# Stores on GpSimd's queue, and a re-ordered passage from up to down, in a hybrid mLSTM/attention block

## The chip, the cores and the metric

The kernel runs on one core of a Trainium2 chip. The metric is the device time of one execution in microseconds (us), smaller is better. The core has five engines, each with its own instruction queue that runs in order: TensorE (PE, matrix products), VectorE (DVE), ScalarE (ACT), GpSimd (POOL) and SyncE (SP). PE writes to PSUM; the others move data between PSUM and the on-chip memory, SBUF. Transfers between SBUF and device memory are done by 16 DMA engines; an engine's queue only issues them. Engines wait for each other by semaphores.

## The reference

One layer of a bidirectional encoder for 2048 tokens of width 1024, in float32:

```
xn   = rms_norm(h, ln_mix_g);  proj = xn @ w_in            # 1024 x 2512
y_a  = mlstm_group(proj[q, k, v, o, gates])                # 4 heads x 128, chunks of 128, both directions
y_b  = mla_group(proj[c_q, c_kv, k_rope])                  # attention, 4 heads, 2048 x 2048 scores each
h    = h + concat(y_a, y_b) @ w_out                        # 1024 x 1024
u    = dwconv3(rms_norm(h, ln_ffn_g) @ w_up)               # 1024 x 5632, then a 3-tap convolution along the tokens
h    = h + (silu(u[gate]) * u[val]) @ w_down               # 2816 x 1024
h    = h + sigmoid(rms_norm(h) @ w_ple_gate) * rms_norm(p @ w_ple_proj)
out  = rms_norm(h, final_g)
```

## The kernel before, in words

**Products.** Every float32 operand is split into a high part and a low part (helper `split`, L112 to L120: ACT casts, DVE subtracts), and each product is three PE passes (`mm3`, L127 to L132). PE is the busiest engine, so all else is arranged around its order.

**Stages.** `run` (L147) calls them in turn.

1. *Input projection* (`in_proj`, L180). x comes turned, in 16 tiles of 128 tokens. `load_w` loads and splits a weight strip; `load_x` (L219) loads an x tile, `split_x` splits it. For the first strip `load_w` loads three weight tiles and then has the first x tile split (`before`). Queries and keys of the mLSTM are made last, feature by feature (`block`, L374); a second stream of work, `side` (weights absorbed for attention, `q_up`), is advanced between products by `pump` (L368) at 0.96 steps a call, and what is left of it runs at the end.
2. *Attention with the mLSTM beside it* (`attend`, L943; `mlstm`, L728). Attention goes over 64 tiles (4 heads, 16 query tiles) in an order written out by hand (`order`, L982). At each dot in it a generator may be advanced by one step; the number of steps is spread evenly with `SIDE` = 613. The generator is the rest of the projection and then the mLSTM: a backward pass over chunks 15 to 1, which stores the turned keys and the state of every chunk (`kn_d`, `cb_d`), and a forward pass over chunks 0 to 15 that reads them back, masks (`affine_select` on POOL, L813), multiplies, normalises (`rsq` on POOL, L135 to L141, then DVE at L860) and stores its part of `y_d` (L867). A `yield` or `pause(n)` marks places where attention's products may go in between. Attention stores its part of `y_d` at L977, two stores for each pair of query tiles.
3. *Output projection* (`out_proj`, L1100): 16 chunks of 128 tokens: 48 products, addition to x, a store of h (`h1_d`, L1135), the norm (root on POOL), and, one chunk later, PE turns the normed tile and `transpose_out` stores it into `x2_d` (L1068; 1024 rows of 512 bytes).
4. *Up and down* (`up_down`, L1359). Both are products of 2 by 2 blocks with seven block products in place of eight (the Winograd form of Strassen's method). The operands are sums and differences: the resident ones are called B11, B21, B22 and T1 to T4 (`load_op`, L1241, loads and splits four 128x512 tiles of each; for later blocks from `t_d` and `tw_d`, where `sum4`, L1205, has stored the sums), the others A11, A12, A22 and S1 to S4 (`up_prep`, L1324). There are 44 up pairs in two blocks of NC2 = 22 (NUP = 44), then 24 down pairs in three blocks of 8. A pair's seven products go A11 by B11, S1 by T1, (rest of the pair before: A22 by T4, S4 by B22), S2 by T2, A12 by B21, S3 by T3; `rest` (L1378) is thus one pair late. `conv` (L1393) is the 3-tap convolution and gate of an up pair: ACT and DVE over two 128x1024 tiles in places w7 and w11, whose result is stored into `hid_d` (L1413, L1415). In the first down pair it comes directly behind `rest` of the last up pair (L1490), and only then are that pair's output tiles loaded (`down_out`). The sums of down's weights (`wsums`, 11 steps) are made at up pairs 28, 31, 34 and 37 and in down's first two blocks (`steps`, L1445).
5. *The per-layer gate and the final norm* (`ple`, L1547), whose preparation runs beside the last down block.

**Queues.** Every DMA, load or store, is issued by SP, so a store waits for its data in the same in-order queue as all loads. A framework decides each engine's order from the program order and its own estimates, allots SBUF by place names (`self.at("w7", ...)`), and puts in the waits for reuse of a place.

Of the kernel before, what the change touches and what calls it, by code (L numbers as in the profile page):

```python
# [19 lines left out]
P = 128  # L20
# [17 lines left out]
SIDE = 613  # L38
# [22 lines left out]
class Block:  # L61
# [118 lines left out]
    def in_proj(self):  # L180
# [6 lines left out]
        def load_w(c0, n, before=None):  # L187

            out, raws = [], []

            def load(k2):
                raw = self.at(next(rrot), [P, 2, 512], name="wraw")
                nc.sync.dma_start(raw[:, :, :n], w_in[k2, :, :, c0:c0 + n])
                raws.append(raw)

            if before:
# [22 lines left out]
        def load_x(st):  # L219

            t = self.at(next(rrot), [P, KT, P], name="x_t")
            for f in range(1 if st else 2):
                fs = slice(0, KT) if st else slice(4 * f, 4 * f + 4)
                nc.sync.dma_start(t[:, fs], d["x_turned"][:, fs, st * P:(st + 1) * P])
            return t
# [72 lines left out]
        ws = load_w(OFF_R, NREST, lambda: split_x(0, xq[0]))  # L298
# [69 lines left out]
        def pump():  # L368
            due[0] += 0.96
# [358 lines left out]
    def mlstm(self):  # L728
# [17 lines left out]
        def state(r, j, kk, v1, old, new):  # L746
# [3 lines left out]
            yield from pause(3)  # L750
# [23 lines left out]
        for c in range(NT - 1, 0, -1):  # L774
# [3 lines left out]
            nc.sync.dma_start(self.kn_d[c], kk[:, 0])  # L778
# [3 lines left out]
            nc.sync.dma_start(self.cb_d[c - 1], new)  # L782
# [3 lines left out]
        for c in range(NT):  # L786
# [3 lines left out]
            cb = self.at(f"t{4 + c % 2}", [P, NH, 129], name="cb")  # L790
            nc.sync.dma_start(cb, self.cb_d[c])
# [9 lines left out]
            if c < NT - 1:  # L801
# [65 lines left out]
            nc.sync.dma_start(self.y_d[c, :, 0:4, :], hy[:, 1])  # L867
# [75 lines left out]
    def attend(self, side):  # L943
# [18 lines left out]
        def pv(w, half):  # L962
# [10 lines left out]
            if half == 1:  # L973
                rb = self.at(f"s{pr % 3}", [P, 2, P], name="ya")
                nc.scalar.copy(rb, w.ps.rearrange("p (a t) -> p a t", a=2))
                for i in range(2):
                    nc.sync.dma_start(self.y_d[2 * pr + i, :, 4 + h, :], rb[:, i])  # L977
# [77 lines left out]
    def transpose_out(self, xn, otag, dst, two=True):  # L1055
# [12 lines left out]
        nc.sync.dma_start(dst, xo)  # L1068
# [31 lines left out]
    def out_proj(self):  # L1100
# [14 lines left out]
        for c in range(NT):  # L1115
# [19 lines left out]
            nc.sync.dma_start(self.h1_d[c], xt)  # L1135
# [69 lines left out]
    def sum4(self, src, dst, ops):  # L1205
# [16 lines left out]
        for i, t in enumerate((b12, b22, b11, b21)):  # L1222
            if not ops or i > 1:
                nc.sync.dma_start(dst(i), t)
# [77 lines left out]
    def down_out(self, i):  # L1302
# [3 lines left out]
        for e in range(2):  # L1306
# [17 lines left out]
    def up_prep(self, i):  # L1324
# [23 lines left out]
        if keep:  # L1348
            nc.sync.dma_start(self.s_d[c, 0], sv)
# [4 lines left out]
        if keep:  # L1354
            nc.sync.dma_start(self.s_d[c, 1], sg)
# [3 lines left out]
    def up_down(self, out):  # L1359
# [4 lines left out]
        L, H = slice(0, SB), slice(SB, 2 * SB)  # L1364
        NUP, blocks = self.NUP, self.BLOCKS
        self.hrot = _rot("", ("u0", "w7", "w11", "u1", "u2"))
# [11 lines left out]
        def rest(s):  # L1378

            prod(s.y, s.ops["A22"], "T4", True)  # L1380
            if s.down:
                add(s.o[1][:, L], s.o[1][:, L], s.y)
                nc.sync.dma_start(self.h2_d[2 * s.pr + 1], s.o[1])
# [3 lines left out]
            if s.down:  # L1387
                add(s.o[0][:, H], s.o[0][:, H], s.z)
                nc.sync.dma_start(self.h2_d[2 * s.pr], s.o[0])
# [3 lines left out]
        def conv(s):  # L1393
            b, c = divmod(s.i, NC2)
            ts = []
            for half, u in enumerate((s.ug, s.uv)):
# [5 lines left out]
                t = self.at(("w7", "w11")[half ^ s.i % 2], [P, 2 * SB], name="fgv")  # L1402
# [9 lines left out]
            if b:  # L1412
                nc.sync.dma_start(self.hid_d[c, :, 2 * SB - 1:4 * SB - 1], ts[0])  # L1413
            else:
                nc.sync.dma_start(self.hid_d[c, :, 0:2 * SB - 1], ts[0][:, 1:])  # L1415
# [27 lines left out]
        sums = [self.sums(1)] + [self.wsums(g) for g in range(3)]  # L1443
        steps = {}
        for q, (i0, at) in enumerate(((0, (6, 9, 12, 15)), (NC2, (6, 9, 12, 15)), (NUP, (2, 3, 4, 5)), (NUP + 8, (2, 3, 4)))):  # L1445
            for a in at:
                steps[i0 + a] = sums[q]
        ple, outs = self.ple(out), {}
        for i in range(n):
# [17 lines left out]
            prod(x, s.ops["A11"], "B11")  # L1467
            if s.down:
                s.o = outs.pop(i) if i in outs else None
            else:  # L1470
                s.p1 = self.at(f"t{6 + i % 2}", [P, SB], name="p1")
                nc.scalar.copy(s.p1, x)
            if s.down and s.o:
                add(s.o[0][:, H], s.o[0][:, H], x)
                o2 = s.o[1].rearrange("p (a t) -> p a t", a=2)
                add(o2, o2, x.unsqueeze(1).broadcast_to([P, 2, SB]))
# [9 lines left out]
            if prev:  # L1486
                rest(prev)
                if prev.i == NUP - 1:
                    conv(prev)
                    s.o = self.down_out(i)  # L1490
                    add(s.o[0][:, H], s.o[0][:, H], x)
                    o2 = s.o[1].rearrange("p (a t) -> p a t", a=2)
                    add(o2, o2, x.unsqueeze(1).broadcast_to([P, 2, SB]))
# [24 lines left out]
            load(then, "B21")  # L1518
# [3 lines left out]
            if s.down and i + 1 < n:  # L1522
                outs[i + 1] = self.down_out(i + 1)
            if prev and not s.down:
                conv(prev)
            prod(s.y, s.ops["S3"], "T3", True)
            if s.down:
# [19 lines left out]
    def ple(self, out):  # L1547
# [99 lines left out]
        for st in range(NT):  # L1647
# [15 lines left out]
            for i in range(len(cuts) - 1):  # L1663
# [9 lines left out]
                nc.vector.tensor_tensor(h2[:, fs], h2[:, fs], gfin[:, fs], op=ALU.mult)  # L1673
            st2 = self.stat(1, "ps3")
            nc.vector.tensor_reduce(st2, s2, axis=AX.X, op=ALU.add)  # L1675
            r2 = self.rsq(st2, 1, 1.0 / D)
# [51 lines left out]
```

## Time and profile before

| | |
|---|---|
| median of 3 runs | 2990.7 us (2990.33 to 2992.8) |
| the profiled execution | 2990.93 us, of which the traced span is 2989.1 us |
| granted TensorE clock, mean | 0.996 |
| DMA issued on SP's queue | 458.12 MB, 47.6% of the 16 engines' time |
| attention with the mLSTM | about 505 to 1250 us of the span |
| output projection, up, down | about 1250 to 1455, 1455 to 2296, 2296 to 2750 us |

How to read the lines that follow: a group row gives line, engine, operation, out<-in; in a timeline row the first two numbers are start and duration in us, xN is how many equal instructions were merged, and the bracket is how long the engine stood idle before, and which instruction or transfer ended the wait. A wait row reads: who <- for whom: us in total, times, longest. "fxy" and "fzs" are PSUM tiles of up and down, "op" a resident operand, "fw" a split operand of a pair, "fgv" a tile of the convolution, "hid_d" the hidden tensor in device memory. SPq is SP's issue queue; its time is that of issuing, not of moving. PEld is the loading of weights into PE, which overlaps PE.

### The profile page before, as it was taken

The numbers are of one execution on the slowest core, as the hardware profiler recorded it, in microseconds if no ns is written. First come the engines' busy times: TensorE is split into PE (matmuls) and PEld (weight loads), VectorE is DVE, ScalarE is ACT, GpSimd is POOL, SyncE is SP. The second block draws the span as 40 slices with busy tenths as digits, with TensorE's granted clock in tenths as the row PEclk, the third lists the DMA queues.
The fourth block names the chain that finished last, engine by engine and source line by source line (L and its number), as shares of the span: only waits on it lengthen the run. The fifth ranks groups of instructions, "written<-read, shape, count | busy, mean of one in ns | idle before, by whom it ended". The sixth has DMA issues, their size and how long they took to land. (4 is left out here: it accounts for less than half of the span.)

```text
span 2989.1 us, 40727 instructions
## 1 busy us (share of the span) xinstructions
PE 2917.3 (98%) x14858; PEld 2452.2 (82%) x14858; DVE 2072.1 (69%) x3798; ACT 1350.2 (45%) x2644; POOL 141.5 (5%) x262
## 2 busy tenths in 40 slices
PE   8999999999999999999999999999997999999999
PEld 7888888889889888888778887788886787877887
DVE  7431556777777777645888888877778778687665
ACT  7211544555656566523544445444445132233443
POOL 3100000000000000001000000000000000000111
PEclk9999999999999999999999999999998999999999
DMA  6522444343333333568663435744436868575221
GB/s 189 115 73 92 138 131 155 119 149 110 100 97 98 94 120 113 168 220 273 217 214 133 141 134 191 250 143 127 123 124 197 274 200 283 190 248 200 79 80 64
DMA packets 377657, 460.73 MB, mean 154 GB/s; under 512 B 30176, under 2 KB 263152, under 8 KB 377456
## 3 DMA queue, kind: packets, MB, share of 16 engines
q1 hardware_dynamic: 377456, 458.12, 47.6%
q8 instruction: 117, 1.92, 0.3%
q14 instruction: 84, 0.69, 0.1%
HBM read 294.53 MB, written 163.51 MB: 153 GB/s over the span
## 5 line engine op out<-in xcount | busy, mean ns | idle before, releaser
L130 PE MATMUL fxy<-op,fw 128*128 128x512 f32 x3168 | 751.3, 393 | 28.7 <-DVE fw L120 16.7
L130 PEld LDWEIGHTS fxy<-op,fw 128*128 128x128 f32 x3168 | 587.4, 188 | 176.2 <-DVE fh L1363 17.8
L130 PE MATMUL fzs<-op,fw 128*128 128x512 f32 x1584 | 385.9, 389 | 0.9 <-DVE xt L1134 0.9
L130 PEld LDWEIGHTS fzs<-op,fw 128*128 128x128 f32 x1584 | 297.1, 188 | 63.0 <-DVE xt L1134 1.1
L130 PE MATMUL bk<-wsp,xh 128*128 128x512 f32 (+1 forms) x768 | 234.9, 387 | 1.2 <-DVE wsp L126 1.0
L117 ACT CAST pt<-tb 128x512 fp32r<-128x512 f32 x256 | 147.1, 587 | 195.5 <-PE tb L959 195.2
L901 DVE TENSOR_REDUCE mx<-bk 128x1 f32<-128x512 f32 x256 | 174.9, 685 | 46.1 <-PE bk L900 44.9
L130 PE MATMUL ppv<-pt,kv 128*128 128x256 f32 x1536 | 203.3, 287 | 0.0
L120 DVE TENSOR_TENSOR pt<-tb,pt 128x512 fp32r<-128x512 f32 x256 | 174.1, 686 | 35.6 <-ACT pt L117 33.9
L130 PE MATMUL fxy<-op,fwd 128*128 128x512 f32 x792 | 191.8, 391 | 6.4 <-DVE fh L1363 3.4
L130 PEld LDWEIGHTS ppv<-pt,kv 128*128 128x128 f32 x1536 | 188.8, 191 | 0.0
L919 ACT ACTIVATE pe<-bk,nm 128x512 f32<-128x512 f32 x256 | 174.5, 696 | 25.5 <-DVE nm L913 24.3
L130 PEld LDWEIGHTS fxy<-op,fwd 128*128 128x128 f32 x792 | 148.0, 188 | 39.9 <-DVE fh L1363 4.9
L130 PE MATMUL pgp<-pw,x3s 128*128 128x512 f32 (+1 forms) x792 | 178.9, 385 | 0.6 <-DVE pw L120 0.6
L130 PE MATMUL bk<-wo,yhl 128*128 128x512 f32 x744 | 175.4, 392 | 0.0
L130 PEld LDWEIGHTS pgp<-pw,x3s 128*128 128x128 f32 x792 | 144.4, 188 | 29.4 <-DVE pw L120 1.1
L130 PEld LDWEIGHTS bk<-wsp,xh 128*128 128x128 f32 x768 | 144.5, 189 | 28.4 <-DVE wsp L126 3.2
L1363 DVE TENSOR_TENSOR fh<-fh,fxy 128x512 f32<-128x512 f32 (+1 forms) x144 | 109.6, 773 | 75.3 <-PE fxy L130 72.8
L130 PEld LDWEIGHTS bk<-wo,yhl 128*128 128x128 f32 x744 | 138.2, 188 | 28.1
L130 PE MATMUL bk<-wsp,xl 128*128 128x512 f32 (+1 forms) x384 | 150.8, 393 | 9.1 <-ACT wsp L125 9.0
L117 ACT CAST fw<-hraw 128x1024 fp32r<-128x1024 f32 (+1 forms) x72 | 70.5, 982 | 192.1 <-PE fxy L130 124.0
L130 PE MATMUL bk<-xh,wqk 128*128 128x512 f32 x480 | 156.8, 392 | 0.0
(325 smaller groups left out, 5019.6 us busy)
## 6 DMA issues: line engine op xcount, KB each, us to landing
fwr<-in_w_up SPq DMA_DIRECT2D x66, 512.0 KB, 4.1
fh<-h_d SPq DMA_DIRECT2D x48, 512.0 KB, 5.1
h_d<-fh SPq DMA_DIRECT2D x48, 512.0 KB, 2.8
s_d<-fwr SPq DMA_DIRECT2D x44, 512.0 KB, 3.1
fws<-s_d SPq DMA_DIRECT2D x44, 512.0 KB, 3.7
rw<-row_d SPq DMA_DIRECT2D x32, 512.0 KB, 5.1
hraw<-hid_d SPq DMA_DIRECT2D x30, 512.0 KB, 4.2
tsum<-in_w_down SPq DMA_DIRECT2D x44, 256.0 KB, 4.5
```

What stands on the lines that cost most here:

```text
L117: nc.scalar.copy(hi, src)
L120: (sub or nc.vector).tensor_tensor(lo, src, _f(hi), op=ALU.subtract)
L130: mm = lambda *a, **k: self.nc.tensor.matmul(*a, **k, skip_group_check=more)
L901: nc.vector.tensor_reduce(s.mx[:, kb:kb + 1], ps, axis=AX.X, op=ALU.max)
L919: nc.scalar.activation(s.pe[:, kb % 2], s.banks[kb], AF.Exp, bias=s.nm, scale=ASCALE, accum_out=s.rs[:, kb:kb + 1])
L1363: add = lambda o, a, b: tt(o, a, b, op=ALU.add)
```

## The change

Line numbers in the prediction are those of the kernel before. The change has these parts:

- *Stores on another queue.* The stores of the mLSTM (`kn_d`, `cb_d`, `y_d`), of attention (`y_d`), of the output projection (`h1_d`, `x2_d`), of `sum4`, of `up_prep` (`s_d`), of `conv` (`hid_d`) and of down (`h2_d`) are issued by GpSimd: 344 stores. SP keeps 970 of 1314 issues. The loads, the projection's stores and the final output stay on SP.
- *The start.* The first two weight tiles are loaded in halves, and one half of the first x tile is loaded and split behind each of them; x's first tile has a place of its own (u2).
- *Side work.* `pump` goes at 0.986 in place of 0.96. `SIDE` is 621 in place of 613. The state update of the backward pass's first chunk pauses 6 steps instead of 3, and the forward pass pauses 5 steps before the first chunk's masks. The state of chunk 0 is not stored and read back.
- *The passage from up to down.* `conv` of the pair before runs behind the products A12 by B21, for every pair, the last up pair included. The first down pair keeps its first partial product in p1, as up pairs do, loads one output tile one pair earlier and the other at its end, and adds the parts (c22). B21 for the next block is loaded behind the products S3 by T3. The order of places for output tiles is another, and the convolution's two tiles no longer swap places from pair to pair.
- *The sums of down's weights* are all made at up pairs 26 to 36, one a pair.
- *The end.* For the last piece of the last chunk the multiplication by the final gain stands behind the reduction.

```diff
-SIDE = 613
+SIDE = 621
...
-            def load(k2):
+            def load(k2, parts=1):
                 raw = self.at(next(rrot), [P, 2, 512], name="wraw")
-                nc.sync.dma_start(raw[:, :, :n], w_in[k2, :, :, c0:c0 + n])
+                for i in range(parts):
+                    bs = slice(2 * i // parts, 2 * (i + 1) // parts)
+                    nc.sync.dma_start(raw[:, bs, :n], w_in[k2, :, bs, c0:c0 + n])
                 raws.append(raw)
...
-                for k2 in range(3):
-                    load(k2)
-                before()
+                load(0, 2)
+                before(0)
+                load(1, 2)
+                before(1)
+                load(2)
+                load(3)
...
+        def first(f):
+            fs = slice(4 * f, 4 * f + 4)
+            if f < 2:
+                nc.sync.dma_start(xq[0][:, fs], d["x_turned"][:, fs, 0:P])
+                self.split(xq[0][:, fs], xh[0][f][:, :, 0:P], xl[0][f][:, :, 0:P])
...
-            due[0] += 0.96
+            due[0] += 0.986
...
-            yield from pause(3)
+            yield from pause(6 if (r, j) == (1, 0) else 3)
...
-            nc.sync.dma_start(self.kn_d[c], kk[:, 0])
+            nc.gpsimd.dma_start(self.kn_d[c], kk[:, 0])
...
-            nc.sync.dma_start(self.cb_d[c - 1], new)
+            if c > 1:
+                nc.gpsimd.dma_start(self.cb_d[c - 1], new)
...
+            if c == 0:
+                yield from pause(5)
...
-            nc.sync.dma_start(self.y_d[c, :, 0:4, :], hy[:, 1])
+            nc.gpsimd.dma_start(self.y_d[c, :, 0:4, :], hy[:, 1])
...
-        nc.sync.dma_start(dst, xo)
+        nc.gpsimd.dma_start(dst, xo)
...
-            nc.sync.dma_start(self.h1_d[c], xt)
+            nc.gpsimd.dma_start(self.h1_d[c], xt)
...
-        self.hrot = _rot("", ("u0", "w7", "w11", "u1", "u2"))
+        self.hrot = _rot("", ("u0", "u2", "u1", "w11", "w7"))
...
-                t = self.at(("w7", "w11")[half ^ s.i % 2], [P, 2 * SB], name="fgv")
+                t = self.at(("w7", "w11")[half], [P, 2 * SB], name="fgv")
...
-                nc.sync.dma_start(self.hid_d[c, :, 2 * SB - 1:4 * SB - 1], ts[0])
+                nc.gpsimd.dma_start(self.hid_d[c, :, 2 * SB - 1:4 * SB - 1], ts[0])
...
-        for q, (i0, at) in enumerate(((0, (6, 9, 12, 15)), (NC2, (6, 9, 12, 15)), (NUP, (2, 3, 4, 5)), (NUP + 8, (2, 3, 4)))):
+        steps = {**{c: sums for c in (6, 9, 12, 15)}, **{NC2 + c: wsums for c in range(4, 15)}}
...
+            if i < NUP + 2:
+                s.p1 = s.spare if i > NUP else self.at(f"t{6 + i % 2}", [P, SB], name="p1")
+                nc.scalar.copy(s.p1, x)
             if s.down:
-                s.o = outs.pop(i) if i in outs else None
+                s.o = outs.pop(i)
+                p1 = s.p1 if i < NUP + 2 else x
+                add(s.o[0][:, H], s.o[0][:, H], p1)
+            if i > NUP:
+                add(twice(s.o[1]), twice(s.o[1]), p1.unsqueeze(1).broadcast_to([P, 2, SB]))
...
                 rest(prev)
-                if prev.i == NUP - 1:
-                    conv(prev)
-                    s.o = self.down_out(i)
...
-            load(then, "B21")
...
+            if prev and not prev.down:
+                conv(prev)
+            if i == NUP - 1:
+                outs[NUP] = self.down_out(NUP, (0,))
+            if i > NUP and i + 1 < n:
                 outs[i + 1] = self.down_out(i + 1)
...
+            if i == NUP:
+                c22 = self.at("t7", [P, SB], name="c22")
+                add(c22, s.p1, s.y)
+                add(c22, c22, s.z)
+                s.o += self.down_out(NUP, (1,))
+                add(s.o[1][:, L], s.o[1][:, L], s.p1)
+                add(s.o[1][:, H], s.o[1][:, H], c22)
...
+            load(then, "B21")
             load(then, "T3")
...
+            if st == NT - 1:
+                nc.vector.tensor_tensor(h2[:, fs], h2[:, fs], gfin[:, fs], op=ALU.mult)
```

More of the change, by code (lines that the diff above doesn't have):

```diff
@@ L219, in load_x @@
         def load_x(st):
[L221 to L224, printed above, removed]
+            t = self.at(next(rrot) if st else "u2", [P, KT, P], name="x_t")
+            if st:
+                nc.sync.dma_start(t, d["x_turned"][:, :, st * P:(st + 1) * P])
             return t
@@ L1300, in down_load, with down_out @@
         self.raw[i] = raw
-    def down_out(self, i):
+    def down_out(self, i, which=(0, 1)):
         g, pr = divmod(i - self.NUP, 8)
         out = []
-        for e in range(2):
+        for e in which:
             t = self.at(next(self.hrot), [P, D], name="fh")
@@ L1442, in up_down @@
         prev, n = None, blocks[-1][0] + blocks[-1][1]
[L1443 to L1447 removed]
+        sums, wsums = self.sums(1), chain(*[self.wsums(g) for g in range(3)])
+        steps = {**{c: sums for c in (6, 9, 12, 15)}, **{NC2 + c: wsums for c in range(4, 15)}}
         ple, outs = self.ple(out), {}
```

42 lines of the change are left out of this document (17 added, 25 removed).

## The prediction

> **What bounds the kernel now.** First the busy times of the page, then who TensorE (PE) waited for.
>
> ```profile
> PE 2917.3 (98%) x14858; PEld 2452.2 (82%) x14858; DVE 2072.1 (69%) x3798; ACT 1350.2 (45%) x2644; POOL 141.5 (5%) x262
> ```
>
> PE is busy for 2917.3 of 2989.1 us. The change keeps every product, so what it can win is a part of the 71.8 us in which PE stood still, and a few slow matmuls after a stop. The view of waits, PE alone, names them (total, times, longest):
>
> ```profile
> PE fxy L130 <- DVE fw L120: 16.7, 2, 15.3
> PE bk L130 <- ACT wsp L125: 9.0, 1, 9.0
> PE fxy L130 <- DVE fh L1363: 8.8, 9, 1.7
> PE fxy L130 <- DVE ug L1363: 5.3, 6, 2.5
> ...
> PE mb L755 <- DVE kk L748: 2.8, 1, 2.8
> PE mb L755 <- DVE cb L759: 1.7, 1, 1.7
> PE tb L612 <- DVE qsr L598: 1.5, 1, 1.5
> ```
>
> One wait of 15.3 us is the largest, the first load (9.0) the next; the rest is small change. The table of windows shows where the large one lies and what a full stage looks like (columns: PE, weight loads, DVE, ACT, POOL, granted clock, DMA share, GB/s):
>
> ```profile
> 1800.00:1900.00 100.00, 95.80 (x415) 76.65 (x414) 88.67 (x119) 56.36 (x83) 0.00 (x0) 1.00 0.65 218
> 2000.00:2100.00 100.00, 100.00 (x441) 82.43 (x441) 70.81 (x84) 43.71 (x57) 0.00 (x0) 1.00 0.40 129
> 2300.00:2350.00 50.00, 33.98 (x138) 26.36 (x139) 38.14 (x54) 12.26 (x16) 0.00 (x0) 0.83 0.77 254
> ```
>
> In the middle of up PE is full. At 2300 to 2350, where up ends and down begins, 16 us are lost, and the granted clock falls to 0.83. The timeline of PE there:
>
> ```profile
> 2292.73 3.06 PE L130 MATMUL fxy<-op,fwd 128*128 128x512 f32 x12 [1.74 <-DVE uv L1363]
> 2295.62 2.88 PE L130 MATMUL fzs<-op,fw 128*128 128x512 f32 x12
> 2313.77 3.35 PE L130 MATMUL fxy<-op,fw 128*128 128x512 f32 x7 [15.27 <-DVE fw L120]
> 2317.77 2.58 PE L130 MATMUL fxy<-op,fw 128*128 128x512 f32 x10 [0.65 <-DVE fh L1363]
> ```
>
> The three waits are 17.7 us. The seven matmuls after the long one take 3.35 us, 0.48 each, the twelve before it 0.24: another 1.7 us. This passage costs 19.4.
>
> **Why it stops there.** ACT and DVE at that place:
>
> ```profile
> 2298.55 1.24 ACT L1403 ACTIVATE fgv<-uv,fcw 128x1024 f32<-128x1024 f32 x1 [0.59 <-DMA hid_d<-fgv]
> 2301.11 1.30 ACT L117 CAST op<-opr 128x512 fp32r<-128x512 f32 x2 [1.33 <-DMA opr<-tw_d]
> ...
> 2308.86 1.22 DVE L1411 TENSOR_TENSOR fgv<-fgv 128x1024 f32<-128x1024 f32 x1
> 2310.00 0.18 DVE L1427 TENSOR_TENSOR hlast<-elast 128x22 f32<-128x22 f32 x1
> 2310.09 2.49 DVE L120 TENSOR_TENSOR op<-opr,op 128x512 fp32r<-128x512 f32 x4
> ```
>
> PE's next product (S2 by T2 of the first down pair) needs the four T2 operands that DVE splits at 2310.09. DVE runs in order, and in front of them stands the convolution of the last up pair, which the old code puts directly behind that pair's last product; its ACT steps wait for the landing of the previous hidden tile and for operand loads, and the end of the sequence (L1411, L1427) passes only at 2310.
>
> **The change part by part.** The sum is made against the profiled execution: 2990.9 us, a span of 2989.1 and 1.8 around it; the median of the runs is 2990.7.
>
> *The passage to down.* The convolution of the last up pair now comes behind the products A12 by B21, half a pair later; the first partial product is kept in a copy (p1), so the output tiles needn't be there; T2's splits no longer stand behind the convolution. The seven sums of down's weights (NUP+2 to 5, NUP+10 to 12) go too. What is late next are operand loads and their splits, as at the other block changes. Up's own, with convolutions beside it, reads by the waits of 1870 to 1895:
>
> ```profile
> PE fxy L130 <- DVE fw L120: 1.5, 1, 1.5
> PE fxy L130 <- DVE uv L1363: 1.1, 1, 1.1
> PE fxy L130 <- ACT p L1472: 0.9, 1, 0.9
> ```
>
> That is 3.5 us. The new code adds four or five additions at the first down pair, each like the rows above some 0.6 us, mostly beside products; I let 1 us of them show. 19.4 less 4.5: a gain of **15** (ends 0 and 19.4).
>
> *mLSTM.* The waits of 2.8 and 1.7 above are its first state update and the start of its forward pass. Three more steps of pause at the first and five at the second put other products in front of the waiting ones, and SIDE rises by the same eight so that the generator still ends with attention. The state of chunk 0 is kept and not stored and read again. Of 4.5 I take **3.5** (0 to 4.5). The side rate of 0.986 in the projection moves the small wait for qsr, 1.5: **0.5** (0 to 1.5).
>
> *The start.*
>
> ```profile
> 1.17 0.97 SPq L224 DMA_DIRECT2D x_t<-in_x_turned  x2
> 2.18 1.03 SPq L193 DMA_DIRECT2D wraw<-in_w_in  x2
> ...
> 8.31 1.26 ACT L125 ACTIVATE wsp<-wraw,gcol 128x464 fp32r<-128x464 f32 x2 [2.69 <-DMA wraw<-in_w_in]
> ```
>
> The first weight tile is cast at 8.31 because both halves of x (512 KB) stand in front of it. Now two weight halves and one half of x come first, 256 KB fewer ahead of the first product; at 218 to 254 GB/s, the rates of the two busy windows above, an estimate of 1.0 to 1.2 us, and the cast begins on half a tile. **1.3** (0 to 2).
>
> *The stores on GpSimd's queue: what they free.* SP issues in order. At 1553 in up:
>
> ```profile
> 1553.13 0.38 SPq L1272 DMA_DIRECT2D fwr<-in_w_up  x1
> 1553.61 0.53 SPq L1415 DMA_DIRECT2D hid_d<-fgv  x1
> ```
> ```profile
> 1558.76 1.25 ACT L1403 ACTIVATE fgv<-uv,fcw 128x1024 f32<-128x1024 f32 x1 [2.74 <-DMA hid_d<-fgv]
> ```
>
> The store of the hidden tile stands behind a weight load, lands late, and the next convolution, which reuses its tile, starts 2.74 us late; DVE and then PE (the longest of the ug waits, 2.5) follow. On a queue of its own the store goes when its tile is ready. **2** (below nothing by 1 us if the new queue lands later, up to the 5.3 of all ug waits). The page "DMA: Bandwidth & Descriptors" of the Trainium skill, section "Issuing engines are not separate DMA queues", says that DMAs of all issuing engines run on the same 16 DMA engines, and that several issuers save only issue time; by it these 2 us would be none and the sum 2 smaller. The rows above show a wait in the issue queue and not a want of engines (DMA share 0.65 at most in up's windows above), so I keep them.
>
> *What they cost.* The trace has no store on POOL. One on SP takes 0.32 to 0.57 us of its queue (rows below); POOL's own small operations take up to 1.01:
>
> ```profile
> 706.51 1.01 POOL L140 TENSOR_TENSOR rsr<-rsm,nhalf 128x4 f32<-128x4 f32 x1
> ```
>
> I take 1 us a store, the nearer row. Behind them wait the reciprocal roots (L138, L140) and the mask select of the mLSTM, on POOL too, and behind these DVE:
>
> ```profile
> DVE hy L860 <- POOL rsr L140: 17.5, 15, 2.3
> ```
>
> DVE already waits 17.5 us for this root, in 15 of 16 chunks, and PE hardly notices. In the order of the changed program, a pair of attention stores stands directly in front of the root in 6 of the 16 chunks, in front of the mask in most others. Six pairs of 2 us are 12 at worst, if none hides; the pairs come every 22 us and the roots every 35, so few meet: a loss of **2** (0 to 12). In up and down POOL has nothing else to do.
>
> *The sums of down's weights* move into up's second half, one in each of 11 pairs instead of 4 there and 7 in down. Seven times four 128x512 operations of about 0.6 us are 17 us more for DVE over 11 pairs of 19 us, 71% busy (second window row) going to 79%: beside PE. In down the same time is freed. **0** (minus 9, see below, to plus 1.5). *The tail:*
>
> ```profile
> 2983.66 0.43 DVE L1673 TENSOR_TENSOR h<-h,gpf 128x256 f32<-128x256 f32 x1 [0.64 <-ACT gate L1672]
> 2984.00 0.15 DVE L1675 TENSOR_REDUCE ps<-ps 128x1 f32<-128x3 f32 x1
> ```
>
> The multiplication by the gain goes behind the reduction and lies beside POOL's root: **0.3** (0 to 0.4).
>
> Sum: 15 + 3.5 + 0.5 + 1.3 + 2 + 0.3 - 2 = 20.6. 2990.9 - 20.6 = **2970**.
>
> **The rivals.**
>
> *A, the passage is bound by its transfers.* Seven operands of four 256 KB tiles are 7.3 MB, with hidden and output tiles 9.8; at the 254 GB/s of the third window 39 us, and PE's work over these two pairs is 38 (168 matmuls at 0.227, from 441 in 100 us). Against it: the 2 MB of sums and their stores that crowded it are gone. If half the stall stays, 10 us, the gain is 11: **2980**.
>
> *B, DVE becomes the bound in up's second half.* The first window row shows it at 88.7% and PE 4.2 us short in 100. If 11 pairs (211 us) ran like that, 9 us go: **2979**. Against: the estimate is 79%, not 89.
>
> *C, slower: GpSimd's queue is too slow in the output projection.* There each chunk issues a store of xt, two root operations and the store of turned tiles, whose 1024 rows of 512 bytes are eight times the rows of any other:
>
> ```profile
> 1277.74 0.32 SPq L1135 DMA_DIRECT2D h_d<-xt  x1
> ```
> ```profile
> 1280.12 0.57 SPq L1068 DMA_DIRECT2D x_d<-nt_o  x1
> ```
> ```profile
> 1289.52 0.32 SPq L1135 DMA_DIRECT2D h_d<-xt  x1
> ```
>
> A chunk lasts 11.8 us. With some 1.6 for the roots, the two stores may take 10.2 before POOL sets the pace, and each us above costs 16, one for each chunk; from 11.5 the 20.6 are eaten and the kernel is slower. If POOL's time goes with the rows, 1 us for 128 and 8 for 1024, the two need 9.1 and just fit; at one and a half times that, 13.7, the loss is 16 times 3.5, or 56: **3026**. For it: nothing in the trace prices rows on POOL. Against: on SP eight times the rows cost 0.57 against 0.32, not eight times.
>
> *D, it doesn't do what it says:* the waits move on and A, B and the worst of the POOL terms come together: about **2990**.
>
> **How the numbers follow.** Forecast 2970, of its own 2962 to 2977: 0.58. A 0.14, B 0.10, C 0.10, D 0.06, and 0.02 for less than 2958 (all gains at their upper ends are 34.6, so 2956). The range 2958 to 2986 takes in the forecast, A and B: 0.82. About 0.2%, 6 us, is what a measurement can tell from no change. Faster by more: forecast, A, B and the low end, 0.84; within: D, 0.06; slower: C, 0.10.
>
> **What would show it.** Right: at the passage no PE wait above 3 us, the ug waits of up near zero, PE's first matmul at 7.5 to 8, the two mLSTM waits gone. POOL's rows with stores show 1 us each, and the roots at most 3 us later than what they wait for. Wrong: a PE wait on DVE at the passage of 8 us or more (A); rows with DVE above 85% and PE below 97 between NC2+4 and NC2+14 (B); stores of turned tiles on POOL above 8 us each, with PE waits for xt in every chunk of the output projection (C).

## The result, and the profile after

The changed kernel takes 3027.95 us, median of 4 runs (3023.24 to 3031.66), beside 2991.75 for the kernel before (4 runs): ratio 1.0121, interval 1.0103 to 1.0139. It is 36 us slower where 21 us faster was forecast. The times and ratios of the experiments leave out one slow run, of f3_reuse_sp, which took 3653.68 us at a granted clock of 0.744.

The page of the changed kernel, busy times:

```profile
PE 2930.8 (97%) x14858; PEld 2460.8 (81%) x14858; DVE 2069.3 (68%) x3799; ACT 1349.7 (45%) x2646; POOL 331.7 (11%) x606
```

PE does the same number of matmuls in a span of 3026.6, so it stands still for 96 us, not 72; its busy time, too, is 13.5 us longer, which fits with slow matmuls behind more stops (in a row below, 15 behind a stop take 5.18 us, 0.35 each, where 0.24 is usual). Its waits (total, times, longest):

```profile
PE fxy L130 <- DVE fh L1380: 19.6, 11, 4.7
PE fxy L130 <- DVE ug L1380: 17.4, 7, 5.2
PE tb L1083 <- DVE xt L1070: 12.1, 6, 4.1
PE bk L130 <- DVE xl L120: 7.4, 1, 7.4
PE fxy L130 <- DVE uv L1380: 4.7, 3, 2.7
...
PE fxy L130 <- DVE fw L120: 3.0, 1, 3.0
PE mb L768 <- DVE kk L761: 2.8, 1, 2.8
...
PE mb L768 <- DVE cb L772: 1.7, 1, 1.7
```

The 15.3 us at the passage are gone, as forecast. In their place stand three groups that were 8.8, 5.3 and 0.8: down's output tiles (fh), up's first half of the gate and value pair (ug), and the rows of the output projection (xt). The table of windows shows two stretches; first the kernel before, then the changed one (PE, weight loads, DVE, ACT, POOL, clock, DMA share, GB/s):

```profile
1250.00:1455.00 205.00, 202.31 (x953) 166.52 (x952) 113.36 (x147) 74.08 (x121) 17.10 (x32) 1.00 0.76 249
...
1870.00:2080.00 210.00, 205.91 (x900) 167.89 (x899) 162.98 (x200) 95.69 (x127) 0.00 (x0) 1.00 0.55 176
```
```profile
1250.00:1455.00 205.00, 190.72 (x889) 155.45 (x888) 100.46 (x133) 68.63 (x112) 42.09 (x74) 0.99 0.69 230
...
1870.00:2080.00 210.00, 184.39 (x770) 147.57 (x769) 161.04 (x210) 82.81 (x113) 29.12 (x54) 0.96 0.72 236
```

In the output projection 64 matmuls fewer fit into the same 205 us, in the stretch with the sums of down's weights 130 fewer into 210. DVE is not fuller in either. So something holds DVE, and PE behind it. The timeline of the output projection, changed kernel:

```profile
1380.73 0.54 POOL L1152 DMA_DIRECT2D h_d<-xt  x1 [1.71 <-DVE xt L1151]
...
1383.08 0.91 POOL L1085 DMA_DIRECT2D x_d<-nt_o  x1 [0.48 <-ACT nt_o L1084]
...
1388.43 1.28 DVE L1070 SCALAR_TENSOR_TENSOR xt<-xt,rsr,g 128x1024 f32<-128x1024 f32 x1 [6.87 <-DMA h_d<-xt]
1389.86 1.10 PE L1083 MATMUL tb<-ident,xt 128*128 128x128 f32 x8 [4.10 <-DVE xt L1070]
```

GpSimd issues the store of a chunk's rows in 0.54 us. DVE then scales the same tile in place and must first see the store land, 7.7 us after its issue; PE's transposes wait 4.1 us for that. Over the whole stage, DVE's waits for this store, before and after:

```profile
DVE xt L1053 <- DMA h_d<-xt: 16.0, 12, 2.5
```
```profile
DVE xt L1070 <- DMA h_d<-xt: 66.7, 15, 8.1
```

The issue rows of the stage's two stores and of one load in the stretch 1250 to 1440 (count, KB each, median us from issue to landing), before and after:

```profile
h_d<-xt SPq DMA_DIRECT2D x16, 512.0 KB, 2.9
x_d<-nt_o SPq DMA_DIRECT2D x15, 512.0 KB, 4.7
...
yr<-y_d SPq DMA_DIRECT2D x11, 512.0 KB, 5.3
```
```profile
h_d<-xt POOLq DMA_DIRECT2D x15, 512.0 KB, 5.8
...
x_d<-nt_o POOLq DMA_DIRECT2D x14, 512.0 KB, 6.8
yr<-y_d SPq DMA_DIRECT2D x11, 512.0 KB, 8.2
```

Both stores land 2 to 3 us later, and here a load on SP's queue, that of y, does too.

In the stretch with the sums, changed kernel:

```profile
1996.52 0.69 DVE L1232 TENSOR_TENSOR tsum<-tsum 128x512 f32<-128x512 f32 x1 [5.85 <-DMA tsum<-in_w_down]
...
2001.99 5.18 PE L130 MATMUL fxy<-op,fw 128*128 128x512 f32 x15 [5.23 <-DVE ug L1380]
```

DVE stands at a sum whose weights have not landed; the additions of the running pair are queued behind, and PE waits 5.2 us for one of them. SP issues such loads late, since it waits for the last sum's store to land (second row); in down it does the same for the output tiles (first row, the same wait before in the fence behind):

```profile
SPq L1325 <- DMA h_d<-fh: 212.6, 41, 10.8
...
SPq L1227 <- DMA tw_d<-tsum: 62.9, 27, 7.6
```
```profile
SPq L1308 <- DMA h_d<-fh: 19.6, 25, 2.1
```

### The profile page after: what moved, and what is told of

The parts are those of the page before. It is cut to its first block, busy times and chain, and to the rows that moved or that the text cites. A ratio compares the mean times of both kernels' runs of the same rounds, so it can differ in the third digit from the quotient of the medians.

```text
span 3026.6 us, 40871 instructions
## 1 busy us (share of the span) xinstructions
PE 2930.8 (97%) x14858; PEld 2460.8 (81%) x14858; DVE 2069.3 (68%) x3799; ACT 1349.7 (45%) x2646; POOL 331.7 (11%) x606
## 5 line engine op out<-in xcount | busy, mean ns | idle before, releaser
L130 PE MATMUL fxy<-op,fw 128*128 128x512 f32 x3168 | 762.5, 397 | 41.9 <-DVE ug L1380 17.4
L130 PEld LDWEIGHTS fxy<-op,fw 128*128 128x128 f32 x3168 | 595.6, 191 | 191.9 <-DVE fh L1380 26.6
```

Source lines behind the costliest of these rows:

```text
L130: mm = lambda *a, **k: self.nc.tensor.matmul(*a, **k, skip_group_check=more)
```

## The experiments

The theory after these readings: a store on the second queue lands later than one on SP's, and it costs where its tile is soon written again ("landing"); the new place of the sums costs by itself ("place"). Rivals: GpSimd's queue is full (C of the prediction); all of the loss is the queue's; stores beside the loads slow the loads ("traffic").

Each run is read by its ratio to the kernel before on the same chip, whose medians beside the runs lie between 2992 and 2998, and by stages: for a given number of recorded matmuls, the time at which a profile has reached it (from windows of 10 us) less the time in the kernel before. The table gives what is lost (plus) or gained within a stage; the stages are matmuls 7600 to 8500, 8500 to 10300, 10300 to 11200, 12300 to 12500 and 12500 to 14800, in the kernel before 1253 to 1440, to 1842, to 2047, 2288 to 2354 and to 2863 us.

| run | ratio, interval | output projection | up, first half | stretch of sums | passage | down and after |
|---|---|---|---|---|---|---|
| changed kernel | 1.0121, 1.0103 to 1.0139 | 12 | -5 | 28 | -7 | 8 |
| e1_sums_old | 1.0111, 1.0088 to 1.0134 | 12 | -5 | 8 | -6 | 24 |
| e2_h1_sp | 1.0091, 1.0069 to 1.0113 | 5 | -5 | 25 | -7 | 13 |
| e3_x2_sp | 1.0112, 1.0087 to 1.0137 | 12 | -5 | 29 | -9 | 9 |
| e4_all_sp | 0.9971, 0.9960 to 0.9983 | 0 | -6 | 6 | -8 | -5 |
| e5_before_pool | 1.0135, 1.0120 to 1.0151 | 14 | -3 | 7 | 2 | 14 |
| f2_attn_pool | 0.9988, 0.9979 to 0.9998 | 0 | -5 | 11 | -8 | -3 |
| f3_reuse_sp | 1.0003, 0.9991 to 1.0014 | 5 | -6 | 11 | -7 | -3 |
| f4_h1_act | 1.0123, 1.0106 to 1.0140 | 12 | -4 | 25 | -6 | 11 |
| g1_best | 0.9975, 0.9961 to 0.9988 | -1 | -6 | 10 | -5 | -7 |
| g2_allsp_sums_old | 0.9938, 0.9913 to 0.9962 | 0 | -5 | -1 | -8 | -2 |
| g3_xn_apart | 1.0098, 1.0066 to 1.0129 | 9 | -5 | 31 | -6 | 8 |
| g4_attn_pool_spread | 0.9972, 0.9958 to 0.9986 | 0 | -6 | 8 | -6 | -5 |
| h1_two_apart | 1.0106, 1.0091 to 1.0121 | 6 | -4 | 31 | -7 | 9 |
| h2_sp_old_sums_old_side | 0.9951, 0.9937 to 0.9965 | -1 | -6 | 3 | -8 | 3 |
| h3_reuse_sp_sums_old | 0.9994, 0.9985 to 1.0003 | 7 | -5 | 7 | -7 | 1 |
| k1_out_pool | 0.9982, 0.9969 to 0.9995 | 12 | -5 | 1 | -8 | 0 |
| k2_out_act | 0.9980, 0.9970 to 0.9990 | 8 | -3 | 1 | -8 | -2 |

What lies ahead, mLSTM and attention, is left out: e4_all_sp and g2_allsp_sums_old have the same instructions there, and their profiles stand 9 us apart at its end (6 behind and 3 ahead of the kernel before). Nothing under that can be read from one profile of it.

**e1_sums_old: the sums back at their old steps.**

```diff
+        late = [NC2 + c for c in (6, 9, 12, 15)] + [NUP + c for c in (2, 3, 4, 5)] + [NUP + 8 + c for c in (2, 3, 4)]
-        steps = {**{c: sums for c in (6, 9, 12, 15)}, **{NC2 + c: wsums for c in range(4, 15)}}
+        steps = {**{c: sums for c in (6, 9, 12, 15)}, **{c: wsums for c in late}}
```

> The changed kernel with the sums of down's weights put back to the steps they had before (four in up's second half three steps apart, four and three in down's first two blocks), all stores left on GpSimd's queue. Theory 'place': counted by matmuls, the changed kernel falls behind the one before by 28 us between 1870 and 2060 us, in the eleven steps that each carry a sum; the sums cost that by their place: 3028 less 28, plus up to 9 us where down's blocks carry seven of them again: 3000 to 3009. Rival 'queue': the sums stall because their stores on GpSimd's queue land late and hold their tiles; then the loss moves with them and the time is 3018 or more.

Measured 3031.13 (its 2996.33 beside it). "Place" alone is refuted: 20 of the 28 us leave the stretch, and 16 come back in down, where the sums now are. With the stores on GpSimd's queue the sums cost wherever they stand.

**e2_h1_sp and e3_x2_sp: one of the output projection's stores back on SP.**

```diff
-            nc.gpsimd.dma_start(self.h1_d[c], xt)
+            nc.sync.dma_start(self.h1_d[c], xt)
```
```diff
-        nc.gpsimd.dma_start(dst, xo)
+        nc.sync.dma_start(dst, xo)
```

> The changed kernel with only the 16 stores of h (the residual rows, line 1152) in the output projection back on SP's queue. Theory 'landing': VectorE scales the same tile in place right behind that store and waits until it has landed (66.7 us in 15 waits, against 16.0 in 12 before), which TensorE's transposes wait for; the 12 us lost between 1380 and 1430 us go: 3016, waits of VectorE for this store below 25 us. Rival C of the prediction (GpSimd's queue is full, with the 1024-row store of the normalized rows the dear one): this store is issued in 0.55 us either way, so nothing changes: 3026 to 3030.

> The changed kernel with only the 15 stores of the normalized rows (line 1085) in the output projection back on SP's queue. Theory 'landing': the store of h stays where it lands late, so most of the 12 us stays: 3022 to 3028. Rival C of the prediction: this store is what fills GpSimd's queue, and the 12 us go: 3016.

The first regains 7 of the 12 us there (3023.46 in all), with this row for DVE in the stage; the second regains nothing (3028.96, and 62.4 us of such waits):

```profile
DVE xt L1070 <- DMA h_d<-xt: 28.4, 13, 4.0
```

Rival C is refuted: the store of 1024 rows is issued in 0.91 us, and putting it back alone regains nothing. So far it looks as if the store whose tile is waited for costs; but with that one back on SP's queue (e2, and f3 and h3 below) 5 to 7 us of this stage are still lost, and in f3 and h3, of h, the sums and the rows, only the 1024 rows are on GpSimd's queue.

**e4_all_sp: every store back on SP's queue.** All 13 lines, as in the two diffs above.

> The changed kernel with all 344 stores back on SP's queue, everything else as changed. Theory 'place and landing': the output projection's 12 us go, the losses of the mLSTM after 1000 us (6 us) and of down (6 to 9 us) go as far as they come from late landing, the sums' 28 us stay: 3000 to 3008. Rival 'queue': all the losses are the queue's, the sums' too: 2965 to 2975.

Measured 2987.84. It lies between the two, 12 us below the one and 13 above the other: against the changed kernel 0.0150 of the ratio, or 45 us, are the queue's. Of the sums' 28 us, 6 stay.

**e5_before_pool: the kernel before, with only the queue changed.** The same lines in the old code, and the state of the last chunk.

> The kernel before with nothing changed but its stores of the mLSTM, attention, output projection, up and down issued on GpSimd's queue. Theory 'queue': the queue alone costs what separates the changed kernel from the same kernel with all stores on SP (3028 against 2988): 2996 plus 25 to 40, with the output projection's 12 us and losses at the sums of up's second half and of down among them. Rival 'together': the queue only hurts where sums stand in eleven steps running; then 2996 plus 12 to 15.

Measured 3031.73, 40 us slower. "Queue" holds, and the losses stand where they stand in the changed kernel: output projection 14, sums 7, down 14.

**f2_attn_pool and f3_reuse_sp: which stores may stay on GpSimd's queue.** The first leaves it y_d, kn_d and cb_d; the second takes h1_d, tw_d with t_d, and h2_d away.

> The changed kernel with only the stores of the mLSTM and of attention left on GpSimd's queue (y_d, kn_d, cb_d), those of output projection, up and down on SP's. Theory 'landing': these stores free nothing that is soon needed, and by the count of matmuls the changed kernel stands 7 us better at the end of attention than the one with all stores on SP: 2988 less 7: 2978 to 2984. Rival: that difference is the order of the attention's side work falling out by chance, and nothing comes of it: 2986 to 2990.

> The changed kernel with those stores back on SP's queue whose tile is written again soon: h in the output projection, the sums' (t_d, tw_d), h in down; the others (y_d, kn_d, cb_d, the normalized rows, hid_d, s_d) stay on GpSimd's. Theory 'landing': a store on GpSimd's queue costs where its tile is waited for, and nowhere else; the out projection's, the sums' and down's losses go: 2980 to 2990. Rival 'traffic': stores on a second queue take the DMA engines from the loads wherever they run, so hid_d and s_d, the larger part of the bytes, go on costing: 3000 or more.

f2: 2987.0, as the rival said: the hoped-for 7 us did not come, which fits with the scatter of the attention told above. f3: 2993.22, just above its forecast by "landing" and under that of "traffic": taking away the stores with reused tiles brings back 35 of the 45 us (1.0121 to 1.0003), not all.

**f4_h1_act: the store of h on ScalarE's queue.**

```diff
-            nc.gpsimd.dma_start(self.h1_d[c], xt)
+            nc.scalar.dma_start(self.h1_d[c], xt)
```

> The changed kernel with only the 16 stores of h in the output projection moved from GpSimd's queue to ScalarE's. 'GpSimd's way of issuing lands late': as with these stores on SP's queue, the output projection regains 7 to 9 us, landing median near 3 us, total 3018 to 3024. 'Any second queue lands late', since a store beside the loads shares the DMA engines with them: landing near 5.5 us, VectorE's waits for it near 67 us, 3026 to 3031.

Undecided: its stores land sooner (3.6 us), DVE waits 34.1 us instead of 66.7, and still the 12 us are lost (3027.83), with the stores of the sums and of the rows left on GpSimd's queue. These waits are near e2's 28.4, and e2 lost 5 there: their sum alone doesn't set the loss.

**g1_best, g2_allsp_sums_old, g4_attn_pool_spread: the place of the sums without the queue.** All stores on SP (g4: but those of mLSTM and attention). g1 and g4 put the sums at every second step of up's second half, g2 at their old steps; g1 has the old side work as well.

```diff
-        steps = {**{c: sums for c in (6, 9, 12, 15)}, **{NC2 + c: wsums for c in range(4, 15)}}
+        late = [NC2 + c for c in range(1, 22, 2)]
+        steps = {**{c: sums for c in (6, 9, 12, 15)}, **{c: wsums for c in late}}
```

> The changed kernel with all stores on SP's queue, the side work of the mLSTM as before (pump 0.96, SIDE 613, the old pauses), and the sums of down's weights one in every second step of up's second half (steps 1, 3 to 21) in place of eleven steps running. By the count of matmuls the run with all stores on SP lost 7 us in mLSTM and attention against the kernel before and 6 us at the sums, and gained 8 at the passage to down, 3 to 5 in down and 6 in up's first half. Theory 'place': without the two losses 2988 less 13: 2972 to 2979. Rival: the sums cost by their transfers, wherever they stand in up, and the attention's order falls out by chance: 2983 to 2990.

> The changed kernel with all stores on SP's queue and the sums of down's weights back at their old steps (four in up, three apart, four and three in down). What the new place of the sums is worth with no store on GpSimd's queue: it costs 6 us in up and gains 3 to 5 in down, so 2988 less 1 to 4: 2984 to 2987. Rival, what the prediction held: the move costs nothing: 2988 or a little more.

> The changed kernel with only the stores of the mLSTM and attention on GpSimd's queue and the sums one in every second step of up's second half. Its sibling with the sums in eleven steps running lost 11 us there: 2987 less 8 to 11: 2976 to 2979. Rival 'transfers': the sums cost it wherever they stand in up: 2984 to 2990.

g1: 2987.96, g4: 2985.05: spreading brings nothing, and my "place" falls in this form too; both meet their rivals. Eleven sums in up's second half cost it 6 to 11 us however they stand. g2: 2974.91, 10 us better than I expected, and the best of all, faster than the kernel before by 0.62% (4 runs, 0.9913 to 0.9962). In its stretch of sums PE waits for nothing but 2.8 and 1.4 us. The windows 1860 to 2060 of e4 and of g2:

```profile
1860.00:2060.00 200.00, 190.80 (x821) 153.53 (x820) 168.65 (x220) 87.24 (x117) 0.00 (x0) 0.99 0.79 253
```
```profile
1860.00:2060.00 200.00, 195.74 (x852) 160.05 (x851) 155.34 (x192) 91.09 (x122) 0.00 (x0) 0.99 0.58 182
```

Seven more sums are 7 times eight transfers of 256 KB, 14.7 MB; the DMA share goes from 0.58 to 0.79 and DVE from 78% to 84%. Which of the two holds PE there wasn't tried by itself.

**g3_xn_apart and h1_two_apart: the tiles taken apart, the stores left on GpSimd's queue.** g3 writes the normalized rows of 13 chunks to a tile of their own; h1 also gives the second and fourth sum of the output projection other tiles (w2, w3, u2, w4).

```diff
-            self.norm_load(xt, g2, self.at(f"t{6 + c % 2}", [P, D], BF16, "junk"))
+            xn = self.at(f"w{c % 2}", [P, D], name="xn") if c < 13 else xt
+            self.norm_load(xt, g2, self.at(f"t{6 + c % 2}", [P, D], BF16, "junk"), xn)
...
-            prev = (xt, "w11", self.x2_d[:, :, c * P:(c + 1) * P])
+            prev = (xn, "w11", self.x2_d[:, :, c * P:(c + 1) * P])
```
```diff
-            r.append(self.at(f"t{i}", [P, SB], name="tsum"))
+            r.append(self.at(tags[i], [P, SB], name="tsum"))
```

> The changed kernel, all its stores on GpSimd's queue, but the normalized rows of the output projection's first 13 chunks are written to a tile of their own instead of over the tile that is being stored. Theory 'landing': the store's late landing costs only because VectorE has to wait for it; the waits go and with them 8 to 12 us: 3016 to 3020. Rival 'traffic': the stores beside the loads slow the output projection's loads, and other waits take their place: 3025 to 3030.

> The changed kernel, all its stores on GpSimd's queue, with both tiles of the output projection that are stored and soon written again taken apart: the normalized rows go to a tile of their own in 13 chunks, and the second and fourth of its four sums use other tiles than the first and third. With the rows alone apart, 8 of the 12 us stayed, in one stall: SP holds the next sum's loads until the last sum's stores have landed, VectorE stands at the sum (4.9 us), TensorE waits 5.6 us for the rows behind it. Theory 'landing on a tile in use': that stall goes too, the output projection loses 0 to 4 us against the kernel before, total 3016 to 3020. Rival 'traffic': loads beside the stores land late themselves, and the sums go on waiting: loss still 8 or more, 3024 to 3029.

"Landing" as I had it is refuted for this stage (the tiles of down and of the sums of its weights were not taken apart). DVE's waits for the store fall to 5.3 us in g3 and 5.1 in h1, but the stage still loses 9 and 6 us (3025.07 and 3032.27). In h1 the waiting is for a load:

```profile
1396.82 0.69 DVE L1100 TENSOR_TENSOR yr<-yr,rb 128x512 f32<-128x512 f32 x1 [6.58 <-DMA yr<-y_d]
...
1406.92 1.94 PE L1083 MATMUL tb<-ident,xn 128*128 128x128 f32 x8 [5.17 <-DVE xn L1070]
```

That load was issued at 1386.11, 10.7 us earlier, and the four stores issued on GpSimd's queue between 1384 and 1392 (h, the normalized rows, two of a sum) land after 7.0 to 8.3 us. The DMA engines are full there (share 0.95 from 1380 to 1398); their line for this time in the same run:

```profile
DMA packets 2478, 6.28 MB, mean 349 GB/s; under 512 B 305, under 2 KB 305, under 8 KB 2476
```

So a load lands late there that shares no tile with these stores. The tiles are not wholly apart, though: SP loads a later chunk's x into the place from which h was stored, and now waits for that store itself, and the loads behind it in the queue wait with it: 21.6 us in g3, and in h1

```profile
SPq L1122 <- DMA h_d<-xt: 36.6, 11, 9.2
```

What part of the 6 to 9 us this makes is not shown.

**h2_sp_old_sums_old_side and h3_reuse_sp_sums_old.** h2 is g2 with the old pump, SIDE and pauses; h3 is f3 with the sums at their old steps.

> All stores on SP's queue, the sums at their old steps, and the side work of the mLSTM as before (pump 0.96, SIDE 613, old pauses): of the change there is left the start, the passage from up to down, the tags, the end. Beside it, the same with the change's side work stood at 2975 (0.9938). 'Side work is worth the 3.5 us of the prediction': 2977 to 2980. 'It is worth nothing or less': 2970 to 2975.

> The changed kernel with the sums at their old steps and with h in the output projection, the sums' stores and h in down on SP's queue; y_d, kn_d, cb_d, the normalized rows, hid_d and s_d stay on GpSimd's. All on SP's queue with the sums there: 2975. Theory 'landing': stores whose tile nobody waits for cost nothing on GpSimd's queue: 2971 to 2979, and where loads no longer stand behind them a little less. Rival 'traffic': they cost wherever loads run beside them: 2983 or more.

h2: 2984.9, above both of its forecasts; 0.9951 beside g2's 0.9938. The intervals overlap, so the worth of the side work stays open. h3: 2996.83 beside a 2997.37, ratio 0.9994, where g2 with those stores on SP's queue has 0.9938. The stores left on the second queue cost some 0.0056, 17 us: "traffic" holds, in the output projection (7), the stretch of sums (7) and little elsewhere. My "nobody waits" was wrong for one of them: SP waits 272 us for the landing of s_d (107 in g2) before it loads the next weights into the same tiles (fwr), but in up's first half, which loses nothing by it. In the two stages that lose, the stores left are the normalized rows and hid_d, and no engine waits long for their tiles.

**k1_out_pool and k2_out_act: the output projection's two stores alone, on GpSimd's or on ScalarE's queue, in g2.** The diff is k1's against g2; k2 has nc.scalar in place of nc.gpsimd.

```diff
-        nc.sync.dma_start(dst, xo)
+        nc.gpsimd.dma_start(dst, xo)
...
-            nc.sync.dma_start(self.h1_d[c], xt)
+            nc.gpsimd.dma_start(self.h1_d[c], xt)
```

> The changed kernel with the sums at their old steps and all stores on SP's queue but the two of the output projection (h and the normalized rows), which stay on GpSimd's. With these two on SP's as well: 0.9938 of the kernel before, and no loss between 1350 and 1440 us. 'A store beside the loads costs where the DMA engines are full': the output projection loses 4 to 12 us, ratio 0.995 to 0.998. If nothing is lost: 0.993 to 0.994.

> The same, with the two stores of the output projection on ScalarE's queue in place of GpSimd's. 'Any second queue': stores and loads share the DMA engines as they do with GpSimd's, so the output projection loses as much as there, within 3 us. 'GpSimd's way of issuing': the loss is gone or below a third of it, ratio within 0.001 of 0.9938.

2993.49 and 2992.95; the ratios 0.9982 and 0.9980 both lie 0.004 above g2's. The output projection loses 12 and 8 us; in no other stage of the table do they differ from g2 by more than 3. The issue rows and DVE's waits, k1 and then k2:

```profile
h_d<-xt POOLq DMA_DIRECT2D x15, 512.0 KB, 5.7
...
x_d<-nt_o POOLq DMA_DIRECT2D x14, 512.0 KB, 6.5
```
```profile
DVE xt L1070 <- DMA h_d<-xt: 58.7, 14, 6.8
```
```profile
h_d<-xt ACTq DMA_DIRECT2D x15, 512.0 KB, 4.0
...
x_d<-nt_o ACTq DMA_DIRECT2D x14, 512.0 KB, 6.9
```
```profile
DVE xt L1070 <- DMA h_d<-xt: 35.3, 13, 6.0
```

Two thirds of the loss come with ScalarE's queue as well, and the ratio isn't near g2's: it is mostly the second queue as such. The 4 us between them are half a us more than the margin I had set, and the store of h lands in 4.0 us instead of 5.7, so up to a third may be GpSimd's own. For the sums and for down, ScalarE's queue was not tried.

## Why the prediction was wrong

**The step that failed** is "What they cost", of the stores on GpSimd's queue. It priced a store by its issue and looked for what is queued behind it on POOL: a loss of 2, at worst 12. That the new queue may land later stands one step before, for the hidden tile alone, at 1 us. The issue was priced well: 0.54 us a store, 0.91 for the 1024 rows, and DVE's waits for POOL's roots in the mLSTM came to 15.7 us (17.5 before). What it left out is when a store lands, and what it takes from the loads. Loads and stores share the DMA engines; the Trainium skill's "DMA: Bandwidth & Descriptors", section "Issuing engines are not separate DMA queues", which I weighed only for the 2 us of gain, says so, and k1 and k2 agree: another issuer brought no faster transfer. The want of engines I had ruled out by windows of up alone (0.65 at most); the output projection was not among them. The kernel before fills the engines there, and PE never stops:

```profile
1380.00:1390.00 10.00, 10.00 (x50) 8.38 (x49) 5.48 (x10) 4.86 (x8) 0.44 (x1) 1.00 0.93 332
1390.00:1400.00 10.00, 10.00 (x50) 8.34 (x49) 6.89 (x11) 3.30 (x6) 1.50 (x2) 1.00 1.00 336
```

So full engines alone don't cost. On SP's queue a load behind a store is issued after it; on two queues they run beside one another, and each lands later where the engines are full. That this order is the reason is argued from these rows, not shown by a run of its own; what GpSimd's queue adds by itself, and in down and at the sums what the tiles in use add, stays open. The cost is 40 us in the old kernel (e5) and 45 in the new (e4), not 2.

**The sums of down's weights**, "0": the step priced 17 us of DVE's time, and none of the 14.7 MB that move with it. On SP's queue the move costs 6 to 11 us in up and gives back 5 in down at most (g1 beside g2); by the ratios (0.9971 against 0.9938) it is about 10 in all, by the stages of e4 and g2 about 4, and the two intervals overlap by a little. With the second queue the stretch loses 28. Rival B had the place and a price of 9, but its mark was not met: PE waited with DVE at 77% (161 of 210 us). On SP's queue alone (e4) it comes near: DVE at 84%, PE at 95%, a loss of 6.

**The passage**, "15": the mechanism was right and the size half. The long wait is gone, and every run that has the new passage gains 5 to 9 us there, with the stores on either queue. What is late next is more than the 3.5 us taken from up's block change; the timeline of PE, changed kernel:

```profile
2340.66 11.17 PE L130 MATMUL fxy<-op,fw 128*128 128x512 f32 x36 [4.31 <-DVE fh L1380]
2353.03 3.01 PE L130 MATMUL fxy<-op,fwd 128*128 128x512 f32 x12 [1.20 <-ACT fzs L1486]
...
2365.24 2.93 PE L130 MATMUL fxy<-op,fw 128*128 128x512 f32 x6 [3.76 <-DVE fh L1380]
```

These are 9.3 us, the two longer ones additions to an output tile that DVE reaches late: at 2340 behind the splits of new operands, at 2363 after a wait of 1.44 us for the tile's load. That is over the 3 us I set as the mark. It is not the queue's: with all stores on SP's the same wait is 8.5 us in e4 and 9.9 in g2.

**mLSTM**, "3.5": not seen. Both waits, 2.8 and 1.7, stand in the list of the changed kernel unchanged; the pauses put nothing in front of them. The wait for qsr, 1.5, went, as forecast at 0.5, and is back in g1 with the old pump. **The start**, "1.3", came at the first matmul: it begins at 7.36 instead of 9.04, and at 7.30 to 8.07 in every run with the new start. Whether it lasts can't be read: at 300 matmuls the changed kernel is 1.2 us ahead, e4 nothing, and e5, with the old start, 0.9.

**The hidden tile's store**, "2": up's first half gains 3 to 6 us in every run, with this store on SP's queue as well (e4: 6) and with nothing but the queue changed (e5: 3). PE's waits for ug from 1440 to 1860 were 4.7 us in the kernel before; they are 0.2 in the changed kernel, 1.9 in e5, and gone in e4. So the queue frees a part of what I said, but some other edit does all of it without the queue; the order of the convolution's tiles is a candidate that was not tried.

**Rival C** gave 3026 and the result is 3028, by another road. It looked for POOL's issue time in every chunk of the output projection; that was under 1 us, the stage lost 12 us, and the rest came from stages it didn't name. A right number here would not have been a right reason.

The sum itself was not far off for a change without the two costs: g2 gains 0.62% of 2991, 18.5 us (interval 11 to 26), where 20.6 were added up. That is in part luck: the passage gives 8 of its 15, up's first half 5 where 2 were set, and the two waits of the mLSTM nothing.

## What to carry to other kernels

Where stores go to a queue of their own, price their landing and what they take from the loads beside them, not their issue; look first for tiles that are written again right behind their store, and for stages that keep the DMA engines busy. With nothing but the queue changed (e5), the stages that had DMA shares of 0.76, 0.62 and 0.59 in the kernel before lost 14, 7 and 14 us, and up's first half, at 0.47, lost nothing. One queue in order may also say what is urgent (argued above, not shown): here it kept the DMA engines busy for 0.76 of the output projection, and PE never waited more than 0.9 us. Work that moves to a stage brings its transfers along; count the bytes per step before and after, as well as the engine time.

## What the runs showed of the hardware

A store of 512 KB issued on GpSimd's queue took 0.54 us of POOL (0.91 with 1024 rows) and landed 3.1 us after its issue in the quiet chunks of g3, where the same store on SP's took 2.9 in the kernel before; beside other transfers, in the changed kernel, it took 5.8 in the median and 7.7 in the row above. So most of the late landing came with the traffic beside it. GpSimd's issue of a store took 0.53 to 0.59 us in the mean at every line of the changed kernel but that of the 1024 rows, so no slow issuing shows. The output projection's two stores, 16.25 MB, went in 4464 packets on GpSimd's queue (k1) and in 17904 on ScalarE's (k2); whether the size of the packets plays a part was not tried by itself. The same code up to the end of attention stood 9 us apart in two profiles (e4, g2), more than several terms of the forecast.
